# Strassen's seven products in the value projection of an encoder's first attention layer

## The chip, the cores and the metric

One core of a Trainium2 chip runs the whole program in one launch. The metric is the device time of one execution in microseconds (us), the median over the runs; one more execution was taken with the hardware profiler.

## The reference

The kernel computes a two-layer encoder on 256 tokens of width 2048, in f32. The first layer is neighbourhood attention with 12 heads of 128 columns, with 4 cross-attention heads into 256 memory tokens beside them; the second has grouped-query attention in place of the neighbourhood one. Each layer ends with a squared-ReLU MLP of width 8192. Cut to the first layer's mixer:

```python
m = rms_norm(mem, mem_norm)
n = rms_norm(h, attn_norm[0])
z = n @ a_w_in[0]                                   # 2048 x (3*1536 + 512)
q, k, v, qm = jnp.split(z, [1536, 3072, 4608], axis=-1)
mix = neighbourhood_attention(q, k, v, a_rpb[0])    # 12 heads, softmax(q k^T * scale + bias + mask) v
km, vm = jnp.split(m @ w_mem_kv[0], 2, axis=-1)
cross = memory_attention(qm, km, vm)                # 4 heads, softmax(qm km^T * scale) vm
h = h + jnp.concatenate([mix, cross], axis=-1) @ w_o[0]
h = h + jnp.square(jax.nn.relu(rms_norm(h, mlp_norm[0]) @ w_up[0])) @ w_down[0]
```

The change concerns `v`, 256 x 1536, of `n @ a_w_in[0]`.

## The kernel before, in words

**Numbers.** Each f32 operand is split into a rounded part (`hi`, made by ScalarE) and the rest (`lo`, a subtraction on VectorE); `split` (L478 to L481) does both. A product is then three matmuls: hi by hi, hi by lo, lo by hi.

**The plan.** All weights come in chunks of 128 x 2048 values (1 MB) through three raw buffers. A chunk is worked off in two halves of 1024 columns, each split into a ring of four `hi` and four `lo` buffers, three halves ahead of their use. The plan, a list of chunks, is built in the order of the computation; `run_all` goes through it half by half, and after every half `tick` (L290) issues what `later` (L287) had put off by a number of halves. From this a scheduler makes the instruction order of each engine when the program is built. An engine works through its own order and never past an instruction that still waits.

**Two kinds of chunk.** An S chunk makes the 128 columns of one head's query, key or memory query: the weights are stationary (128 x 128) and 256 tokens move, 16 blocks by three matmuls (L385), into one PSUM bank, `ps_s`. An M chunk is four blocks of the value or output projection: the activations are stationary and 512 weight columns move, 4 blocks by 2 token halves by three matmuls (L362, L365, L366), into two banks, `ps_m`. PSUM has eight banks; four are for such sums (`acc`) and four for the attention's own tiles (`att`).

**The first layer's part.** Once the memory's keys and values are there, the plan holds 4 memory-query chunks, and then three groups (`GH`) of four heads. A group is 4 M chunks for the values of its four heads (256 x 512), then a query and a key chunk for each head. When a query chunk is done, `a_q_done` scales it by 1/rms of the token out of PSUM (`summed`, L525, on VectorE, which frees the bank) and splits it; `a_k_done` does the same for the key and starts the attention of that head at the next tick. `a_v_done` scales and splits the group's values (L670 on ScalarE, L671 on VectorE, `va`).

**An attention** has four steps, put off by 1, 2, 4 and 5 ticks. `attend`: scores by six matmuls (L537 to L539), bias added (L546), the maximum (L548), the exponential on ScalarE, the reciprocal of the sum (L553), and the scaling by it, two instructions on VectorE (L555). `turned`: two transposes on VectorE (L592) and a DMA. `halved`: the split of the probabilities `pT_t`. `attend3`: six matmuls with the values (L611 to L613), and the split of the result into `cat`.

**Later parts** are the output projection, and the MLP, which already works with seven products for eight there, with its sums of weights by GpSimd's accumulating DMAs (L1073) and by VectorE (L1076).

Of the kernel before, what the change touches and what calls it, by code (L numbers as in the profile page):

```python
# [10 lines left out]
F32 = mybir.dt.float32  # L11
# [6 lines left out]
P = 128  # L18
D = 2048
# [39 lines left out]

LONGER = {"hi": 128, "lo": 128}  # L60

# [86 lines left out]


class Grain:  # L150


    def __init__(self, run, after=None, load=None, pre=None, prep=None, ahead=(8, 5, 3)):
# [4 lines left out]
def encoder_kernel(ctx: ExitStack, tc: tile.TileContext, t: dict, out: bass.AP):  # L158
# [35 lines left out]
    def open_work():  # L194
        at.work = opened("work", side="right", bufs=2)

    open_sums()
    open_ring()
    open_work()

    first = const.tile([P, GAINS + NT * D], F32, name="first")
    gains, mem0 = first[:, :GAINS], first[:, GAINS:]
    h = mem0.rearrange("p (a b) -> p a b", a=NT)
    raws = [at.ring.tile([P, CH], F32, tag="raw", bufs=3, name=f"raw{c}") for c in range(FIRST_CHUNKS)]


    def load_mem(j):
        s = slice(GAINS + j * 512 if j else 0, GAINS + (j + 1) * 512)  # L210
        nc.sync.dma_start(first[:, s], t["mem_rest"][j - 1] if j else t["mem_first"])
# [26 lines left out]
    def gain(which, k):  # L238
        return gains[:, which * KT + k : which * KT + k + 1]

# [149 lines left out]
    def begin():  # L390

        box["memT"] = at.cat.tile([P, KT, 512], F32R, tag="cat", name="memT")
        tiles = {}
        for w in plan[:FIRST_CHUNKS]:
# [134 lines left out]
    def attend(qT, kT, bias=None):  # L529
# [120 lines left out]
    def get(name):  # L650
        return lambda: box[name]
# [14 lines left out]
    def head_of(v, hd):  # L666
        return lambda part, kt: v[:, part, kt, hd * HD : (hd + 1) * HD]

# [81 lines left out]

    def x_load():
        for i in range(NT):
            pin(nc.sync.dma_start(h[:, i, :], t["x"][i * P : (i + 1) * P, :]))
        box["xT"] = []
        for a in range(2):
            y = at.work.tile([P, 8, SEQ], F32, tag="l4", name="xT")
            pin(nc.sync.dma_start(y.rearrange("p a b -> p (a b)"), t["xT"][:, a * XW // 2 : (a + 1) * XW // 2]))
            box["xT"].append(y)

# [12 lines left out]
    def x_norm(j):  # L772
        if j == 0:
            box["nT"] = wide("nT0", 480)
        for k in (2 * j, 2 * j + 1):
            split_pair(box["nT"], box["xT"][k // 8][:, k % 8, :], G_A0, k)

# [20 lines left out]
    def a_k_done(hd):  # L798
        def f(w):
            k = at.work.tile([P, 512], F32R, tag="b_y2", name="kT")  # L800
            s = summed(w.ps, "k", box["x_row"])
            split(k[:, :SEQ], k[:, SEQ:], s)
            b = at.work.tile([P, BJ * GRID_W], F32, tag="b_o", bufs=3, name="bias")
            nc.sync.dma_start(b, t["bias"][hd])
            attention([(box.pop(("q", hd)), k, b, head_of(box["v", hd // GH], hd % GH), hd, box["cat"])], 1)
        return f
# [10 lines left out]

    for hd in range(NMH):
        add_s(t["w_aqm"][hd], get("nT"), a_qm_done(hd))
# [26 lines left out]
    def o_done(layer, nb):  # L846
# [40 lines left out]
        def f(w):  # L887
            if nb == 0:
                closed("work")
                at.side = opened("side", side="right")  # L890
# [289 lines left out]
    def plain_grains(layer, nb, at_chunk):  # L1180
# [19 lines left out]
        def begin():  # L1200
            if nb == REST[0]:
                closed("ps_sums")
                open_sums(layer)
# [290 lines left out]
    later(21, x_load)  # L1494
    for j in range(8):
        later(24 + j, x_norm, j)
    later(25, x_stats)
    run_all()
# [27 lines left out]
def m_chunks(w):  # L1526

    k, n = w.shape
    x = w.reshape(k // D, 4, 4, P, n // 512, 512).transpose(0, 4, 1, 3, 2, 5)
    return np.ascontiguousarray(x).reshape(-1, P, CH)  # L1530

# [113 lines left out]
```

## Time and profile before

| | before |
|---|---|
| median of 3 runs | 2002.28 us (2002.08 to 2002.89) |
| the profiled execution's own time | 2002.73 us |
| its span, first to last instruction | 2001.0 us |
| mean granted TensorE clock | 0.999 |
| TensorE (PE) busy | 1989.8 us |
| VectorE (DVE) busy | 1718.8 us |
| ScalarE (ACT) busy | 1329.9 us |
| GpSimd (POOL) busy | 123.0 us |

The first layer's projections and attention lie at 95 to 334 us of the span.

Times in the profile are microseconds from the span's start. PE is TensorE, PEld its weight loads, DVE is VectorE, ACT ScalarE. A row of a group gives line, engine, operation, result and operand by the names in the program, the shape, the count, then busy time and mean duration in ns, then the idle time just ahead of these instructions. Matmuls overlap in the pipeline, so that their pitch, from start to start, tells what one costs, and not its duration.

### The profile page before, as it was taken

How to read it: one execution, taken by the hardware profiler on the slowest of the kernel's cores; microseconds unless marked ns; L12 is line 12 of the kernel's file. 1: busy time of each engine (PE TensorE's matmuls, PEld its weight loads, DVE VectorE, ACT ScalarE, POOL GpSimd, SP SyncE). 2: the span in 40 equal slices, each digit the busy share in tenths (PEclk: the TensorE clock that was granted, in tenths of full speed). 3: DMA queues.
4: the chain of work that ended last, by engine and by line, in shares of the span. 5: the costliest groups of instructions: out<-in, count | busy, mean ns of one | idle time of the engine just before them, and what ended most of it. 6: DMA issues, size and time to landing. Idle time of an engine off the chain costs nothing.

```text
span 2001.0 us, 32691 instructions
## 1 busy us (share of the span) xinstructions
PE 1989.8 (99%) x12920; PEld 1806.7 (90%) x12920; DVE 1718.8 (86%) x2080; ACT 1329.9 (66%) x1849; POOL 123.0 (6%) x145
## 2 busy tenths in 40 slices
PE   9999999999999999999999999999999999999998
PEld 8999999899999999999998888889999999999997
DVE  6777777589998999999999779778998999999997
ACT  6655555477777777677766556667776777777774
POOL 0000000000000000000000001000000000000000
PEclk9999999999999999999999999999999999999999
DMA  7866655767777777777666765568777777777772
GB/s 294 310 196 207 209 198 191 257 205 233 239 225 231 232 234 237 237 229 227 213 226 208 238 222 171 190 197 259 229 223 239 226 226 238 233 236 234 220 235 102
DMA packets 105562, 448.02 MB, mean 224 GB/s; under 512 B 10944, under 2 KB 38336, under 8 KB 58048
## 3 DMA queue, kind: packets, MB, share of 16 engines
q1 hardware_dynamic: 88416, 414.99, 59.2%
q0 software_dynamic: 16704, 30.42, 9.5%
q8 instruction: 101, 1.65, 0.3%
q10 hardware_dynamic: 288, 0.52, 0.1%
q14 instruction: 53, 0.43, 0.1%
HBM read 398.17 MB, written 4.19 MB: 201 GB/s over the span
## 4 chain that ended last, share of the span: by engine, by line
PE 98%; DVE 1%; issue 0%; DMA 0%; ACT 0%; SPq 0%; DVEq 0%; POOLq 0%; POOL 0%; ACTq 0%
PE ps_u L385 35%; PE ps_s L385 10%; PE p L1106 9%; PE p L1104 9%; PE p L1107 9%; PE ps_m L362 8%; PE ps_m L365 8%; PE ps_m L366 8%; PE sc_ps L538 0%; PE av L612 0%; PE sc_ps L539 0%; PE sc_ps L537 0%; PE av L611 0%; PE av L613 0%; DMA raw<-in_w_first 0%
## 5 line engine op out<-in xcount | busy, mean ns | idle before, releaser
L385 PE MATMUL ps_u<-hT,uh 128*128 128x256 f32 x3812 | 663.6, 276 | 0.0
L385 PEld LDWEIGHTS ps_u<-hT,uh 128*128 128x128 f32 x3812 | 578.9, 188 | 5.5
L385 PE MATMUL ps_u<-hT,ul 128*128 128x256 f32 x1960 | 541.5, 276 | 0.0
L480 ACT ACTIVATE uh<-raw_U 128x1024 fp32r<-128x1024 f32 x262 | 276.7, 1058 | 209.3 <-PE ps_u L385 195.7
L385 PEld LDWEIGHTS ps_u<-hT,ul 128*128 128x128 f32 x1960 | 368.0, 188 | 0.0
L481 DVE TENSOR_TENSOR lo<-raw,hi 128x1024 fp32r<-128x1024 f32 (+1 forms) x215 | 254.7, 1190 | 101.2 <-ACT hi L480 100.1
L481 DVE TENSOR_TENSOR ul<-raw_U,uh 128x1024 fp32r<-128x1024 f32 x262 | 318.4, 1219 | 15.6 <-ACT uh L480 15.4
L480 ACT ACTIVATE hi<-raw 128x1024 fp32r<-128x1024 f32 (+1 forms) x215 | 221.6, 1036 | 162.1 <-PE ps_m L366 86.7
L481 DVE TENSOR_TENSOR tl<-t,th 128x2048 fp32r<-128x2048 f32 x116 | 265.6, 2290 | 71.4 <-ACT th L480 71.0
L480 ACT ACTIVATE th<-t 128x2048 fp32r<-128x2048 f32 x116 | 222.7, 1920 | 117.4 <-PE p L1107 114.8
L481 DVE TENSOR_TENSOR bl<-b,bh 128x1536 fp32r<-128x1536 f32 x116 | 203.2, 1752 | 0.0
L1104 PE MATMUL p<-th,a_s 128*128 128x512 f32 x464 | 181.2, 391 | 0.0
L1106 PE MATMUL p<-tl,a_s 128*128 128x512 f32 x464 | 181.0, 390 | 0.0
L1107 PE MATMUL p<-th,a_s 128*128 128x512 f32 x464 | 180.5, 389 | 0.0
L480 ACT ACTIVATE bh<-b 128x1536 fp32r<-128x1536 f32 x116 | 172.4, 1486 | 7.9
L1073 POOL DMA_DIRECT2D t<-b x116 | 101.0, 871 | 1143.9 <-ACT t L1072 1060.7
L385 PE MATMUL ps_s<-nT,hi 128*128 128x256 f32 x896 | 154.7, 276 | 0.0
L1107 PE MATMUL p<-bh,a_s 128*128 128x512 f32 x348 | 136.2, 391 | 0.0
L1106 PE MATMUL p<-bl,a_s 128*128 128x512 f32 x348 | 135.7, 390 | 0.0
L385 PEld LDWEIGHTS ps_s<-nT,hi 128*128 128x128 f32 x896 | 135.5, 188 | 0.2
L1104 PE MATMUL p<-bh,a_s 128*128 128x512 f32 x348 | 135.4, 389 | 0.0
L385 PE MATMUL ps_s<-nT,lo 128*128 128x256 f32 x448 | 123.7, 276 | 0.0
(296 smaller groups left out, 3590.7 us busy)
## 6 DMA issues: line engine op xcount, KB each, us to landing
raw_U<-in_w_up SPq DMA_DIRECT2D x128, 1024.0 KB, 5.5
b<-in_w_pair SPq DMA_DIRECT2D x116, 1024.0 KB, 5.7
raw<-in_w_o SPq DMA_DIRECT2D x32, 1024.0 KB, 5.0
t<-b POOLq DMA_DIRECT2D x116, 256.0 KB, 5.2
raw<-in_w_b SPq DMA_DIRECT2D x21, 1024.0 KB, 5.2
raw<-in_w_av SPq DMA_DIRECT2D x12, 1024.0 KB, 4.9
raw<-in_w_aq SPq DMA_DIRECT2D x12, 1024.0 KB, 4.9
raw<-in_w_ak SPq DMA_DIRECT2D x12, 1024.0 KB, 4.8
```

The costliest lines, as they stand in the source:

```text
L362: first = nc.tensor.matmul(ps, ah, hi[:, s], start=st, stop=False)
L365: nc.tensor.matmul(ps, ah, lo[:, s], start=False, stop=False)
L366: final = nc.tensor.matmul(ps, al, hi[:, s], start=False, stop=sp)
L385: ins = nc.tensor.matmul(ps, x, acts[:, k, part], start=k == n == 0, stop=k == KT - 1 and n == 2)
L480: first = nc.scalar.activation(dst_hi, src, AF.Copy)
L481: return first, nc.vector.tensor_tensor(dst_lo, src, dst_hi.bitcast(F32), op=ALU.subtract)
L1073: nc.gpsimd.dma_start(s[:, 3, :], b[:, 1, :], accum_op=ALU.add)
L1104: ins = nc.tensor.matmul(ps, a[:, 0, ai, :], hi[:, s], start=begins, stop=False)
L1106: nc.tensor.matmul(ps, a[:, 0, ai, :], lo[:, s], start=False, stop=False)
L1107: nc.tensor.matmul(ps, a[:, 1, ai, :], hi[:, s], start=False, stop=ends)
```

## The change

**The products.** A 512-row, 512-column piece of the value weights is taken as two pairs of row blocks by two halves of 256 columns. For each pair the 2 x 2 block product (token halves by row blocks, row blocks by column halves) is made with Strassen's seven products `p1` to `p7`, each 128 tokens x 128 rows x 256 columns, in place of eight. A chunk has two such pairs, so 7 x 2 x 3 = 42 matmuls of 256 columns in place of 24 of 512. The seven products of a group add up over its four chunks in four banks, `ps_v`, two products to a bank.

**The operands.** Four of the products need sums of activations: `x_sums` makes them, one call for each of the four row ranges (four additions of 256 columns and a split of 1024). Four need sums of weights: `pre` makes them for each chunk with one ScalarE copy, two GpSimd accumulating DMAs of 256 KB and two VectorE additions of 512 columns. What is split for a chunk is the raw 2048 columns (half chunk one: `p3`, `p1`, `p2`, `p5`) and 1536 columns of sums (half chunk two: `p7`, `p6`, `p4`).

**The results.** `values_done` combines the products of a group out of PSUM by one ScalarE copy and seven VectorE additions of 256 columns (`v_c`), then scales and splits as before (now L693, L694).

**The order of the plan.** The value chunks of a group no longer stand ahead of it: of the 24 half chunks (three groups of four chunks, in the order 2, 0, 1, 3) one stands behind each of the 28 memory-query, query and key chunks in turn, two behind the fifth and the sixth, until they are used up.

**PSUM.** In the first layer `acc` has five banks and `att` three. While a group's values are open, four of the five hold `ps_v`, and one is left for `ps_s`.

**Besides.** In the first layer the attention's scaling goes from VectorE to ScalarE. The activations are normed in pairs of blocks, by ScalarE and then a split. `x` is loaded after its transposed copy, and once more, 2 MB, after the last group's values, since its room holds sums of activations in between. The unused columns behind `hi` and `lo` shrink from 128 and 128 to 32 and 64.

The core of the diff:

```diff
-        for x in ("acc", "att")[:: 1 if layer else -1]:
-            setattr(at, x, opened(f"ps_{x}", space=bass.MemoryType.PSUM, bufs=4))
+        for x, n in (("acc", 5 - layer), ("att", 3 + layer))[:: 1 if layer else -1]:
+            setattr(at, x, opened(f"ps_{x}", space=bass.MemoryType.PSUM, bufs=n))
...
-            nc.vector.tensor_scalar(sc[:, s, :], sc[:, s, :], rs[:, s : s + 1], None, op0=ALU.mult)
+            if box["layer"]:
+                nc.vector.tensor_scalar(sc[:, s, :], sc[:, s, :], rs[:, s : s + 1], None, op0=ALU.mult)
+            else:
+                nc.scalar.activation(sc[:, s, :], sc[:, s, :], AF.Copy, scale=rs[:, s : s + 1])
...
+    def x_sums(c):
...
+        for n, a, b, op in ((0, x[:, :, 0], x[:, :, 2], ALU.subtract), (1, x[:, :, 0], x[:, :, 1], ALU.add),
+                            (2, d[:, :, 0], x[:, :, 1], ALU.add), (3, x[:, :, 3], d[:, :, 2], ALU.subtract)):
+            nc.vector.tensor_tensor(d[:, :, n], a, b, op=op)
+        split(res[:, :, 0], res[:, :, 1], d)
...
-    def a_v_done(g):
-        def f(w):
-            box["v", g] = values("l4", "va")
-            put_values(box["v", g], w.ps, box["x_col"])
-        return f
+    PARTS = (("p3", "p1", "p2", "p5"), ("p7", "p6", "p4"))
...
+    def value_grains(g, c, begins, ends):
...
+        def pre():
+            b = own["b"].rearrange("p (a b) -> p a b", a=4)
+            s = own["t"] = at.spare.tile([P, 3, 512], F32, tag="sums", name="v_t")
+            nc.scalar.activation(s[:, 2, :], b[:, 2, :], AF.Copy)
+            nc.vector.tensor_tensor(s[:, 0, :], b[:, 3, :], b[:, 0, :], op=ALU.add)
+            nc.gpsimd.dma_start(b[:, 3, :], b[:, 1, :], accum_op=ALU.add)
+            nc.vector.tensor_tensor(s[:, 1, :], s[:, 0, :], b[:, 1, :], op=ALU.add)
+            nc.gpsimd.dma_start(s[:, 2, :], s[:, 1, :], accum_op=ALU.add)
...
+        def run(n):
+            if begins and n == 0:
+                box["v_ps"] = [at.acc.tile([P, 512], F32, tag="acc", name="ps_v") for _ in range(4)]
+            for m in range(2):
+                hi, lo = own.pop((n, m))
+                for q in range(2):
+                    for a, name in enumerate(PARTS[n][2 * m : 2 * m + 2]):
...
+                        for part, x, st, sp in ((0, hi, begin and half == 0, False), (0, lo, False, False),
+                                                (1, hi, False, end)):
+                            ins = nc.tensor.matmul(ps, left(name, q, part), x[:, s], start=st, stop=sp,
+                                                   skip_group_check=True)
...
+    def values_done(g):
...
+        nc.scalar.activation(c[:, 0, 0], p["p1"], AF.Copy)
+        for d, x, y, op in ((c[:, 1, 0], p["p2"], c[:, 0, 0], ALU.add), (c[:, 1, 1], p["p6"], c[:, 0, 0], ALU.subtract),
+                            (c[:, 0, 1], c[:, 1, 1], p["p7"], ALU.subtract), (c[:, 0, 0], c[:, 0, 1], p["p4"], ALU.add),
+                            (c[:, 0, 1], p["p5"], c[:, 0, 1], ALU.subtract),
+                            (c[:, 1, 1], c[:, 1, 1], p["p5"], ALU.subtract), (c[:, 1, 1], c[:, 1, 1], p["p3"], ALU.add)):
+            nc.vector.tensor_tensor(d, x, y, op=op)
+        box["v", g] = values("l4", "va")
+        put_values(box["v", g], [c[:, i].rearrange("p a b -> p (a b)") for i in range(NT)], box["x_col"])
+        if g == NH // GH - 1:
+            h_load()
...
-    for g in range(NH // GH):
-        add_m([t["w_av"][g * 4 + c] for c in range(4)], parts_of("nT"), a_v_done(g))
-        for hd in range(g * GH, (g + 1) * GH):
-            add_s(t["w_aq"][hd], get("nT"), a_q_done(hd))
-            add_s(t["w_ak"][hd], get("nT"), a_k_done(hd))
+    CHUNKS = (2, 0, 1, 3)
+    with_values = [x for g in range(NH // GH) for n, c in enumerate(CHUNKS) for x in value_grains(g, c, n == 0, n == 3)]
...
+    for n, (src, done) in enumerate(projections):
+        add_s(src, get("nT"), done)
+        for _ in range(1 + (n in (4, 5))):
+            if with_values:
+                plan.append(with_values.pop(0))
```

**The order of the instructions, before and after.** Each engine's order is fixed when the program is built. Numbers behind a name tell one buffer from another; `x2` stands for two instructions that follow each other.

On TensorE, before, at the key chunk `ps_s_1866` of the second head (its key is `kT_1921`) the next chunk `ps_s_1961` follows, and the head's scores `sc_ps_1937` stand at that next chunk's end:

```order
L385 MATMUL ps_s_1961<-nT0_920,hi_1893 128x256 x2
L611 MATMUL av_1928<-pT_t_1822,va_1635 128x256
L537 MATMUL sc_ps_1937<-kT_1921,qT_1855 128x256
L538 MATMUL sc_ps_1937<-kT_1921,qT_1855 128x256
L539 MATMUL sc_ps_1937<-kT_1921,qT_1855 128x256
...
L612 MATMUL av_1928<-pT_t_1822,va_1635 128x256
L613 MATMUL av_1928<-pT_t_1822,va_1635 128x256
L385 MATMUL ps_s_1961<-nT0_920,lo_1894 128x256
L385 MATMUL ps_s_2033<-nT0_920,hi_1957 128x256 x2
```

After, the second head's key chunk is `ps_s_2099` and its key `kT_2160`; the half chunk of values behind it works on `ps_v_2065` and `ps_v_2066`:

```order
L404 MATMUL ps_s_2099<-nT0_926,hi_2059 128x256 x2
L404 MATMUL ps_s_2099<-nT0_926,lo_2060 128x256
L557 MATMUL sc_ps_2167<-kT_2160,qT_2045 128x256
L558 MATMUL sc_ps_2167<-kT_2160,qT_2045 128x256
L559 MATMUL sc_ps_2167<-kT_2160,qT_2045 128x256
...
L559 MATMUL sc_ps_2167<-kT_2160,qT_2045 128x256
L882 MATMUL ps_v_2065<-hi_2091,left_1028 128x256
L882 MATMUL ps_v_2065<-lo_2092,left_1028 128x256
```

The scores stand directly behind the last matmul of the key that they need, and ahead of the half chunk of values.

On TensorE after the change, in the steady part of the second group, the key chunk `ps_s_2565` is followed by the next head's query chunk `ps_s_2689`:

```order
L404 MATMUL ps_s_2565<-nT0_926,lo_2521 128x256
L404 MATMUL ps_s_2565<-nT0_926,hi_2520 128x256 x2
L404 MATMUL ps_s_2565<-nT0_926,lo_2521 128x256
L404 MATMUL ps_s_2689<-nT0_926,hi_2598 128x256 x2
L404 MATMUL ps_s_2689<-nT0_926,lo_2599 128x256
```

Two S chunks in a row stood there before as well; now `ps_v` holds four of the five banks, so that both are in the same bank. Eight such pairs stand in the order.

On VectorE, before, where group 0's values (`va_1635`) are made out of `ps_m`:

```order
L481 TENSOR_TENSOR lo_1643<-raw_1640,hi_1642 128x1024
L481 TENSOR_TENSOR cat0_1154<-av_1557,cat0_1154 128x256
L671 SCALAR_TENSOR_TENSOR va_1635<-ps_m_1472,x_col_965,va_1635 128x512
L671 SCALAR_TENSOR_TENSOR va_1635<-ps_m_1473,x_col_965,va_1635 128x512
L481 TENSOR_TENSOR lo_1672<-raw_1640,hi_1671 128x1024
```

After, with the query `q_s_2046` of the second head, taken out of `ps_s_1986`, among the combinations `v_c_1964`:

```order
L903 TENSOR_TENSOR v_c_1964<-v_c_1964,ps_v_1227 128x256
L545 SCALAR_TENSOR_TENSOR q_s_2046<-ps_s_1986,x_row_999 128x256
L903 TENSOR_TENSOR v_c_1964<-ps_v_1225,v_c_1964 128x256
L903 TENSOR_TENSOR v_c_1964<-v_c_1964,ps_v_1225 128x256
L501 TENSOR_TENSOR lo_2018<-raw_2015,hi_2017 128x1024
L903 TENSOR_TENSOR v_c_1964<-v_c_1964,ps_v_1224 128x256
L501 TENSOR_TENSOR lo_2060<-raw_2015,hi_2059 128x1024
L501 TENSOR_TENSOR pT_t_1937<-pT_t_1937 128x512
L501 TENSOR_TENSOR qT_2045<-q_s_2046,qT_2045 128x256
L694 SCALAR_TENSOR_TENSOR va_1973<-v_c_1964,x_col_993,va_1973 128x512 x2
```

Three of the seven combinations and both writes of `va_1973` now stand behind the reading of a query chunk that ends one S chunk later than the group's products. The first matmuls with these values, `av_2050`, stand on TensorE directly behind that S chunk, `ps_s_1986`.

More of the change, by code (lines that the diff above doesn't have):

```diff
@@ L58 @@
 ENTRY_AT = 192
[L60 removed]
+LONGER = {"hi": 32, "lo": 64}
+LEFT = 16
 COPY_AT = 384
@@ L147, in __getitem__ @@
         return self.rest[:, s.start - P : s.stop - P] if s.start else self.first
+class Rows:
+    def __getitem__(self, key):
+        return self.now[key]
 class Grain:
+    kind, last_block = "G", False
     def __init__(self, run, after=None, load=None, pre=None, prep=None, ahead=(8, 5, 3)):
@@ L238, in gain @@
     def gain(which, k):
-        return gains[:, which * KT + k : which * KT + k + 1]
+        src = first[:, LEFT:] if which == G_MEM else gains
+        return src[:, which * KT + k : which * KT + k + 1]
     box: dict = {"layer": 0}
@@ L392, in begin @@
         box["memT"] = at.cat.tile([P, KT, 512], F32R, tag="cat", name="memT")
+        later(1, lambda: nc.scalar.activation(gains, first[:, LEFT : LEFT + GAINS], AF.Copy))
         tiles = {}
@@ new lines, in values_done @@
+    def values_done(g):
+        p = {name: box["v_ps"][bank][:, half * SEQ : (half + 1) * SEQ] for name, (bank, half) in PLACES.items()}
+        c = at.work.tile([P, NT, 2, SEQ], F32, tag="pT", name="v_c")
+        nc.scalar.activation(c[:, 0, 0], p["p1"], AF.Copy)
[7 more added lines that the diff above has]
+        if g == NH // GH - 1:
+            h_load()
@@ L888, in f @@
             if nb == 0:
+                if not layer:
+                    closed("spare")
                 closed("work")
@@ L1494, in encoder_kernel @@
     later(21, x_load)
-    for j in range(8):
-        later(24 + j, x_norm, j)
-    later(25, x_stats)
+    for n, j in enumerate((4, 5, 0, 1, 2, 3, 6, 7)):
+        later(24 + n, x_norm, j)
+    for n, c in zip((27, 29, 31, 34), CHUNKS):
+        later(n, x_sums, c)
+    later(26, x_stats)
     run_all()
```

96 lines of the change are left out of this document (77 added, 19 removed).

## The prediction

> **What bounds the kernel now.** I read the page first (the span, the engines' busy time and the chain that ended last).
>
> ```profile
> span 2001.0 us, 32691 instructions
> PE 1989.8 (99%) x12920; PEld 1806.7 (90%) x12920; DVE 1718.8 (86%) x2080; ACT 1329.9 (66%) x1849; POOL 123.0 (6%) x145
> PEclk9999999999999999999999999999999999999999
> PE 98%; DVE 1%; issue 0%; DMA 0%; ACT 0%; SPq 0%; DVEq 0%; POOLq 0%; POOL 0%; ACTq 0%
> ```
>
> TensorE sets the end: 99% busy and 98% of the chain, at full granted clock in every slice. Only fewer TensorE microseconds can shorten this kernel, and every wait of TensorE lengthens it. Then the windows, for the first layer's projections and for a stretch of its MLP (columns: PE, PEld, DVE, ACT, POOL, clock, DMA share, GB/s):
>
> ```profile
> 95.00:334.00 239.00, 239.00 (x1808) 227.40 (x1808) 176.36 (x272) 125.13 (x202) 0.00 (x0) 1.00 0.62 206
> 600.00:900.00 300.00, 300.00 (x2023) 275.30 (x2022) 277.18 (x289) 214.68 (x249) 25.32 (x29) 1.00 0.75 233
> ```
>
> In the stage of the change TensorE is busy in 239.00 of 239.00 us: no wait is there to be removed. VectorE has 176.36 of 239 (74%). In the MLP it has 277.18 of 300 (92%), and TensorE still never waits, so that a load of 92% can be carried if the order leaves room.
>
> **What the products save.** The matmuls' pitch, from the list of TensorE's instructions in order of time (start, duration):
>
> ```profile
> 136.03 0.39 PE L366 MATMUL ps_m<-hi,nT 128*128 128x512 f32 x1
> ...
> 136.71 0.39 PE L366 MATMUL ps_m<-hi,nT 128*128 128x512 f32 x1
> ...
> 150.85 0.28 PE L385 MATMUL ps_s<-nT,lo 128*128 128x256 f32 x1
> 150.96 0.39 PE L385 MATMUL ps_s<-nT,hi 128*128 128x256 f32 x2
> 151.19 0.28 PE L385 MATMUL ps_s<-nT,lo 128*128 128x256 f32 x1
> ```
>
> Three matmuls of 512 columns take 136.71 − 136.03 = 0.68 us, .2267 each; three of 256 take 151.19 − 150.85 = 0.34, .1133 each: exactly half. The value projection has 12 chunks x 24 = 288 of the one kind, 65.3 us, and gets 12 x 42 = 504 of the other, 57.1 us. **Term 1: −8.2 us.** If the new matmuls ran at the pitch of the scores (rows below: .117), 504 x .004 = 2 us of it would be lost; I take the S chunk's pitch, since shape and way of loading are its own.
>
> The Trainium skill, "TensorE: Matmul & The Clock Gate", section "Wait — 56ns, not 53.3ns?", gives each warm matmul a fixed part of about 2.5 ns beside its columns. By it the 216 matmuls more would take an estimated .5 us of the saving back; the two pitches above, exactly 2 to 1, show no such part.
>
> **What the sums cost.** VectorE's durations, in a stretch where it runs without gaps:
>
> ```profile
> 244.48 0.69 DVE L546 TENSOR_TENSOR sc<-sc_ps,bias 128x512 f32<-128x512 f32 x1
> 245.19 0.42 DVE L525 SCALAR_TENSOR_TENSOR q_s<-ps_s,x_row 128x256 f32<-128x256 f32 x1
> 245.53 1.22 DVE L481 TENSOR_TENSOR lo<-raw,hi 128x1024 fp32r<-128x1024 f32 x1
> 246.66 0.68 DVE L548 TENSOR_REDUCE nm<-sc 128x2 f32<-128x512 f32 x1
> 247.26 0.41 DVE L481 TENSOR_TENSOR cat<-av,cat 128x256 fp32r<-128x256 f32 x1
> 247.59 0.41 DVE L481 TENSOR_TENSOR qT<-q_s,qT 128x256 fp32r<-128x256 f32 x1
> ...
> 249.24 1.15 DVE L592 STREAM_TRANSPOSE sc_t<-sc 128x256 f32<-128x256 f32 x2
> 250.31 1.18 DVE L481 TENSOR_TENSOR lo<-raw,hi 128x1024 fp32r<-128x1024 f32 x1
> ```
>
> From start to start: .34 for 256 columns, .60 for 512, 1.14 for 1024, 1.07 for both transposes. One head of the changed stage (query, key, one value chunk) then asks of VectorE: S splits 4 x 1.14 = 4.6; value splits 3 x 1.14 + .60 = 4.0; sums of weights 2 x .60 = 1.2; q, k and `cat` 5 x .34 = 1.7; the rest of the attention 3 x .60 + 1.07 + .2 for the reciprocal (a rounded-up .17) = 3.1; a quarter of `values_done`, (7 x .34 + 2 x .7)/4 = .9. Together 15.5 us. TensorE needs 96 x .1133 + 42 x .1133 + 12 x .12 = 17.1 us. That is 91%, the MLP's load: VectorE alone doesn't become the bound. In the stretch from the first memory query to the second head's query the order holds, with the sums of activations, 25 subtractions of 1024, 22 operations of 512, 26 of 256, 10 transposes and 5 reciprocals, 56.9 us, against 58.1 of TensorE (6 S chunks of 5.44, 4 value chunks of 4.76, 54 attention matmuls): 98%, tight.
>
> The accumulating DMAs and the reload lie beside this:
>
> ```profile
> L1073 POOL DMA_DIRECT2D t<-b x116 | 101.0, 871 | 1143.9 <-ACT t L1072 1060.7
> t<-b POOLq DMA_DIRECT2D x116, 256.0 KB, 5.2
> ```
>
> 24 issues of .87 us on a GpSimd that is idle here (0.00 in the window), each landing in 5.2 us. A value chunk comes round every 17 us, its raw data three steps ahead of use. Two DMAs in turn make 2 x (5.2 + .9) = 12 us, which the rest of a period covers with 5 us left; without that cover each chunk would cost the excess. The 2 MB of `x` at the end wait behind nothing that TensorE needs before the output projection, and the ScalarE copies and scalings go to an engine with 125 of 239 us busy. All three at nothing.
>
> **What the order costs.** Before, a head's scores stand amid the chunk after the next matmuls, so that nothing waits:
>
> ```profile
> 231.40 0.28 PE L385 MATMUL ps_s<-nT,hi 128*128 128x256 f32 x1
> 231.52 0.28 PE L538 MATMUL sc_ps<-kT,qT 128*128 128x256 f32 x1
> 231.64 0.28 PE L539 MATMUL sc_ps<-kT,qT 128*128 128x256 f32 x1
> ...
> 231.99 0.28 PE L539 MATMUL sc_ps<-kT,qT 128*128 128x256 f32 x1
> 232.11 0.28 PE L385 MATMUL ps_s<-nT,hi 128*128 128x256 f32 x1
> 232.31 0.69 DVE L546 TENSOR_TENSOR sc<-sc_ps,bias 128x512 f32<-128x512 f32 x1 [0.35 <-PE sc_ps L539]
> 5.20 0.69 DVE L481 TENSOR_TENSOR lo<-raw,hi 128x512 fp32r<-128x512 f32 x1
> 5.95 0.39 PE L385 MATMUL ps_s<-memT,lo 128*128 128x256 f32 x1 [0.23 <-DVE lo L481]
> ```
>
> These give the two handovers: from TensorE's last matmul to a waiting VectorE 232.31 − 231.99 = .32, which is .20 after the next matmul could have started (231.99 + .12); from VectorE's end, 5.20 + .69 = 5.89, to TensorE at 5.95, .06. After the change TensorE, which never steps past a waiting instruction, meets four kinds of wait; each is a sum of these rows, with VectorE and ScalarE just in time.
>
> A. *Scores directly behind the chunk that they need.* For the second key (the first place of the order) VectorE reads `k_s` (.34), subtracts `lo_2186` (1.14, it stands between) and then `kT` (.42): .20 + .34 + 1.14 + .42 + .06 = 2.16, less .12 for the one matmul that goes ahead, 2.0. The first key has a 512 between: 1.5. The first memory query has .34, 1.14, .34 between: .20 + .34 + 1.82 + .42 + .06 less two matmuls, 2.6. The second has 1.14, 1.14, .60 between, less eight matmuls: 3.0. At the fifth key `av_3032` stands ahead of the scores, and ahead of its `pT_t` (.69) stand 1.14 and .60: .20 + .34 + 1.74 + .69 + .06 less two matmuls, 2.8. Sum 11.9.
>
> B. *One bank for two S chunks.* TensorE may not start the second before VectorE has read the first: .20 + .42 + .06 = .68, eight times, 5.4.
>
> C. *Group 0's values behind a query* (the third place). From the end of `ps_s_1986`: .20, then .34 for the query, 3 x .34 + 2 x 1.14 + .60 + .34 in VectorE's order, .66 for the first `va` and .75 for the second to be there, .06:
>
> ```profile
> 215.33 1.40 DVE L671 SCALAR_TENSOR_TENSOR va<-ps_m,x_col,va 128x512 fp32r<-128x512 f32 x2
> ```
>
> 6.2 us, less .5 for the matmuls of the first half: 5.7.
>
> D. *`ps_s_1816`* (first key) needs a `lo` that stands seven places behind the first query's reading on VectorE: .20 + .34 + 1.14 + .60 + 1.07 + .34 + .60 + .34 + 1.22 + .06 = 5.9, of which 31 matmuls between hide 3.5: 2.4.
>
> **Term 2: +11.9 + 5.4 + 5.7 + 2.4 = +25.4.** VectorE isn't just in time, though: it finishes what it has in hand. The trace of before has no such wait, so I bound it: nothing, or one 1024 subtraction (1.14) at each of the 15 waits, 17. I take half of one at each, as nearest to a queue 91 to 98% full. **Term 3: +8.5.** A later wait also gives VectorE time to catch up, which is why I don't go above it.
>
> Sum on the profiled execution: its own time 2002.73 − 8.2 + 25.4 + 8.5 = 2028.4. That execution was .45 over the median of the runs, so 2028.0.
>
> **The rivals.**
>
> *Faster: the waits are covered.* If the handovers of A, C and D overlapped with work that the order hides from me (matmuls of other banks ahead of the waiting ones), only B would be left: 2002.3 − 8.2 + 5.4 = 1999.5; with B covered too, 1994.1. It decides from the point where all waits together are under 8.2. Against it: each chain above begins with the last matmul of a chunk and ends at the very next instruction. 5%.
>
> *VectorE as the bound in the tight stretch alone.* If scores and values waited little but the 98% stretch could be run only at the MLP's 92%, it would take 56.9/.92 = 61.8 in place of 58.1, +3.7: 2002.3 − 8.2 + 3.7 = 1997.8. For it: the MLP row. Against it: the same as above. 4%.
>
> *The granted clock falls after long waits.* C, the second memory query and the fifth key with lateness hold waits of 3 to 6 us, which the trace of before has nowhere; its clock is full in all 40 slices. If it halved for one S chunk after each of two such waits, 2 x 5.44 = 11 us more: 2039.0. The Trainium skill, the same page, section "What's actually happening" in Part 1, has such a gate, with a window of about 3.4 us; the trace of before, without such an idle stretch, can't show it. 10%.
>
> *The forecast*, 80%; 1% for something else, on the slow side.
>
> **The numbers.** 2028.0. Low: term 3 at nothing and a third of term 2 covered, 2028.0 − 8.5 − 8.5 = 2011.0; high: term 3 whole (+8.5) and the scores' pitch (+2), 2038.5, drawn out to the clock's rival, 2039.0. About 4.0 us (0.2%) either way is what a measurement of this kernel can tell from no change. Of the two fast rivals (9%) I give half to each side of that bound: faster .05, same .04, slower .91.
>
> **What would show it.** In TensorE's waits of the changed kernel: the five scores of A behind VectorE's or ScalarE's `kT`, `qmT`; eight waits of about .7 for VectorE's `k_s` or `qm_s`; one of about 6 for `va`; TensorE's busy time less by 8, VectorE in the stage near 91%. I am wrong if these waits sum to under 12 us, if the matmuls at L882 have a pitch other than .113, or if the clock leaves 1.00.

## The result, and the profile after

The changed kernel takes 2049.64 us, median of 4 runs (2049.11 to 2050.81), against 2002.55 us of the kernel before beside it: a ratio of 1.0236, 95% interval 1.0218 to 1.0254. It is slower, as forecast, but by 47 us where 26 were forecast, and outside the range (2011 to 2039). Its page, the rows that answer to those shown of before:

```profile
span 2047.6 us, 33383 instructions
PE 2006.2 (98%) x13136; PEld 1826.6 (89%) x13136; DVE 1760.5 (86%) x2126; ACT 1376.8 (67%) x1933; POOL 144.3 (7%) x169
PEclk9988999999999999999999999999999999999999
PE 92%; DVE 3%; DMA 2%; issue 1%; ACT 1%; SPq 0%; DVEq 0%; POOL 0%; POOLq 0%; ACTq 0%
```

TensorE is busy for 16.4 us more, although it has 8 us less to do: two slices with a granted clock of 8 tenths are new. The chain has VectorE, DMA and ScalarE in it now. Nearly all of it is in the stage of the change (the window's columns: PE, PEld, DVE, ACT, POOL, clock, DMA share, GB/s; then TensorE's waits there: us in total, times, longest):

```profile
95.00:345.00 250.00, 219.00 (x1735) 213.72 (x1734) 187.27 (x272) 141.31 (x233) 19.01 (x22) 0.95 0.67 203
```

```profile
PE sc_ps L557 <- ACT qmT L500: 6.5, 2, 4.3
PE ps_s L404 <- DVE k_s L545: 4.6, 6, 1.5
PE av L634 <- ACT pT_t L500: 3.9, 2, 3.4
PE av L634 <- ACT va L693: 3.3, 1, 3.3
PE sc_ps L557 <- ACT kT L500: 3.2, 2, 1.9
PE ps_s L404 <- DVE qm_s L545: 3.0, 2, 1.8
PE av L635 <- DVE pT_t L501: 2.1, 3, 0.9
PE ps_s L404 <- DVE lo L501: 2.1, 1, 2.1
...
```

These are the forecast's waits by name: scores for `qmT` and `kT`, eight S chunks for the reading of their bank (`k_s` six times, `qm_s` twice), one for `lo`, `av` for `va` and `pT_t`. VectorE is busy in 187.27 of 250 us, 75%: it is not the bound.

The longest wait, 4.33 us at the first memory query, has a cause of its own. The query's last matmul starts at 101.57; behind it, on ScalarE and VectorE:

```profile
102.34 2.00 ACT L500 ACTIVATE hi<-raw 128x1024 fp32r<-128x1024 f32 x2 [4.01 <-DMA raw<-in_w_aqm]
105.25 0.42 DVE L545 SCALAR_TENSOR_TENSOR qm_s<-ps_s,x_row 128x256 f32<-128x256 f32 x1
```

ScalarE waits 4.01 us for the next chunk's weights to land, VectorE's subtractions stand behind ScalarE's rounding, and the query is read at 105.25, some 3.4 us later than in the forecast's chain.

The second head's key, in TensorE's and VectorE's lists (start, duration):

```profile
201.00 0.28 PE L404 MATMUL ps_s<-nT,lo 128*128 128x256 f32 x1
202.62 0.38 PE L557 MATMUL sc_ps<-kT,qT 128*128 128x256 f32 x1 [1.34 <-ACT kT L500]
203.90 0.38 PE L558 MATMUL sc_ps<-kT,qT 128*128 128x256 f32 x1 [0.90 <-DVE kT L501]
204.12 0.34 PE L559 MATMUL sc_ps<-kT,qT 128*128 128x256 f32 x1
```

```profile
201.32 0.42 DVE L545 SCALAR_TENSOR_TENSOR k_s<-ps_s,x_row 128x256 f32<-128x256 f32 x1 [0.63 <-PE ps_s L404]
202.29 1.23 DVE L501 TENSOR_TENSOR lo<-raw,hi 128x1024 fp32r<-128x1024 f32 x1 [0.55 <-ACT hi L500]
203.43 0.42 DVE L501 TENSOR_TENSOR kT<-k_s,kT 128x256 fp32r<-128x256 f32 x1
```

This is the forecast's chain: VectorE reads at 201.32, .32 after the last matmul; the subtraction of 1024 that stands between starts .55 late, because ScalarE's rounding was late; `kT` follows at 203.43 and TensorE goes on at 203.90. From 201.00 to 204.12 there are three matmuls, .34 us of work: 2.8 us lost, forecast 2.0 and a part of term 3.

Now the clock, in windows of 3.41 us (busy us of TensorE with its matmuls first, the granted clock third from the end):

```profile
101.83:105.25 3.42, 0.01 (x1) 0.00 (x0) 1.81 (x4) 2.00 (x2) 0.00 (x0) 0.99 1.07 352
105.25:108.66 3.41, 1.59 (x5) 1.30 (x6) 2.62 (x7) 1.48 (x2) 0.00 (x0) 0.50 0.70 231
108.66:112.07 3.41, 3.41 (x17) 3.41 (x17) 1.93 (x3) 1.35 (x5) 0.00 (x0) 0.50 0.67 276
132.60:136.00 3.40, 1.63 (x14) 1.46 (x13) 2.50 (x4) 2.00 (x3) 0.00 (x0) 1.00 0.74 284
136.00:139.40 3.40, 3.40 (x32) 3.40 (x31) 0.68 (x2) 1.39 (x2) 0.00 (x0) 1.00 0.76 251
170.07:173.48 3.41, 1.54 (x10) 1.34 (x11) 3.38 (x6) 1.51 (x3) 0.32 (x1) 1.00 0.74 240
173.48:176.89 3.41, 3.41 (x19) 3.41 (x17) 1.78 (x4) 1.47 (x4) 1.41 (x2) 0.50 0.89 206
```

A window at full clock in which TensorE was busy for .01 or 1.54 us is followed by one at half clock (17 to 19 matmuls where 32 fit); one with 1.63 us is not. The window with 1.59 us is itself at half clock, and another follows it. The edges lie on one grid: 112.07, 125.76, 176.89 and 207.65 are 4, 15 and 9 times 3.41 apart. Eight windows of the stage are at half clock, behind the five waits of A and behind C.

Where the 46.6 us of span went. Adding up, for each matmul of the stage, the time to the next one's start less .1133 us per 256 columns:

| | forecast | measured |
|---|---|---|
| products (term 1) | −8.2 | −8.2 (no row against it) |
| A, scores behind their chunk | 11.9 | 19.8 |
| B, one bank, eight times | 5.4 | 8.9 |
| C, group 0's values | 5.7 | 5.6 |
| D, `ps_s_1816` | 2.4 | 2.4 |
| one more wait, for `pT_t` | | 0.7 |
| lateness (term 3, in A to D when measured) | 8.5 | |
| matmuls at half clock | 0, a rival of 10% | 9.7 |
| matmuls at .118 where .1133 was taken | 0, bound 2 | 4.4 |
| the rest: 1.2 ahead of the stage, .5 behind the output projection, 1.6 not assigned | | 3.3 |
| sum | 25.7 | 46.6 |

The waits come to 37.4 us where terms 2 and 3 had 33.9. The rows for half clock and for the pitch of .118 are what the forecast lacked.

### The profile page after: what moved, and what is told of

Its sections match the earlier page's. It is cut to its first block, busy times and chain, and to the rows that moved or that the text cites. A ratio compares the mean times of both kernels' runs of the same rounds, so it can differ in the third digit from the quotient of the medians.

```text
span 2047.6 us, 33383 instructions
## 1 busy us (share of the span) xinstructions
PE 2006.2 (98%) x13136; PEld 1826.6 (89%) x13136; DVE 1760.5 (86%) x2126; ACT 1376.8 (67%) x1933; POOL 144.3 (7%) x169
## 4 chain that ended last, share of the span: by engine, by line
PE 92%; DVE 3%; DMA 2%; issue 1%; ACT 1%; SPq 0%; DVEq 0%; POOL 0%; POOLq 0%; ACTq 0%
PE ps_u L404 34%; PE p L1230 9%; PE p L1228 9%; PE p L1231 9%; PE ps_s L404 7%; PE ps_m L381 6%; PE ps_m L385 6%; PE ps_m L384 6%; PE ps_v L882 2%; DVE lo L501 1%; DMA mem_k<-km_w 1%; DMA raw<-in_w_aqm 1%; ACT hi L500 0%; PE av L635 0%; PE av L636 0%
## 5 line engine op out<-in xcount | busy, mean ns | idle before, releaser
L404 PE MATMUL ps_s<-nT,hi 128*128 128x256 f32 x896 | 159.9, 279 | 7.5 <-DVE k_s L545 4.6
```

Source lines behind the costliest of these rows:

```text
L404: ins = nc.tensor.matmul(ps, x, acts[:, k, part], start=k == n == 0, stop=k == KT - 1 and n == 2)
```

## The experiments

The theory: **order**. TensorE loses its time at handovers that the order of the instructions forces, each priced as above, and to the half clock that follows where they leave a window too empty. Its rivals: **load** (VectorE's added work makes the waits, wherever they stand) and **products** (the value matmuls themselves don't save). The kernel before ran beside all of them, 2002.5 to 2002.8 us.

### scores_behind: before, with the scores behind their chunk

```diff
-        products(w.ps, w.acts(), k0, nk, hi, lo)
+        products(w.ps, w.acts(), k0, nk, hi, lo, keep_order="nT" in box and not box["layer"])
```

> The kernel before, with its products for eight, four banks and no sums, but with the S chunks' matmuls of the first layer kept in the order of the plan: the scores of 9 heads and 3 memory heads then stand directly behind the chunk that they need. Theory (order): 12 waits of .20 + .34 + 1.14 + .42 + .06 = 2.2 us, some less, 20 to 28 us, and after the longer ones a halved clock, 0 to 20 us more: 2022 to 2050, granted clock in that stage under 1.00. Rival (load): VectorE has 74% in that stage here, so that it catches up, under 2008.

Measured: 2044.39 us, ratio 1.0210 (1.0194 to 1.0226). TensorE's waits in the stage, and its window:

```profile
PE sc_ps L537 <- ACT kT L480: 9.1, 9, 1.4
PE sc_ps L538 <- DVE kT L481: 7.8, 9, 0.9
PE sc_ps L537 <- ACT qmT L480: 4.5, 3, 1.7
PE sc_ps L539 <- DVE qmT L481: 1.1, 2, 0.8
```

```profile
95.00:375.00 280.00, 257.26 (x1807) 240.34 (x1806) 182.38 (x275) 125.98 (x203) 0.00 (x0) 0.96 0.52 175
```

Twelve heads, 22.5 us of idling (29 from start to start), and 12 us of matmuls at half clock: +42, without a single product, sum or bank of the change. VectorE has 65% there. Order holds, load falls for this kernel. Two windows of this run show that the busy time alone doesn't tell which window is followed by a slow one:

```profile
263.59:267.00 3.41, 1.81 (x13) 1.42 (x12) 2.23 (x4) 1.11 (x3) 0.00 (x0) 1.00 0.33 91
267.00:270.41 3.41, 3.41 (x18) 3.41 (x18) 2.18 (x6) 1.10 (x4) 0.00 (x0) 0.50 0.82 334
```

Here 1.81 us were too little, where 1.63 were enough in the changed kernel. The matmuls that start in a window tell it better: 11 here, 12 there. Over the windows at full clock of eleven runs (from 60 us on, a matmul of 512 columns counted twice), all 46 with up to 11 starts were followed by a halved one and none with 13 or more; of the three with 12, two were.

### one_bank: before, with one bank for S chunks in a row

```diff
         def start(w):
+            if "nT" in box and not box["layer"] and plan[plan.index(w) - 1].acts is acts:
+                w.ps = box["ps_s"][:, :SEQ]
+                return
...
```

> The kernel before, in which the S chunks of the first layer that follow each other all use one PSUM bank; nothing else changed. Theory (order and banks): three groups have seven such handovers and the memory queries some, 20 in all, each .20 + .42 + .06 = .68 us: +13.6, about 2016, and as each wait is short the clock stays at 1.00. Rival (load): VectorE has a quarter of its time free, within 4 us of before.

Measured: 2022.49 us, ratio 1.0101 (1.0088 to 1.0115), +20 where 13.6 were expected. The clock row stays at 1.00.

```profile
PE ps_s L385 <- DVE k_s L528: 5.5, 9, 0.6
PE ps_s L385 <- DVE q_s L528: 4.9, 9, 0.6
PE ps_s L385 <- DVE qm_s L528: 1.1, 2, 0.6
```

Twenty waits, as counted; from start to start they cost 14.9 us, .74 each, and one for `pT_t` .9. The other 4 are S matmuls, .1165 on the mean, in a kernel whose buffers are those of before. About 1.8 of it lies directly behind the handovers, where the first matmul takes .08 to .11 longer; of the rest about a third run at .117 to .119, so that the slower pitch comes with such handovers as well.

### sums_alone: before, with the work of the sums on scratch

```diff
                 box["weights"] = split(*tiles[hf], src)
+                if "a_v_done" in w.done.__qualname__:
+                    more(src)
...
+    def more(src):
+        a = at.spare.tile([P, 3, 768], F32, tag="more", name="more")
+        nc.vector.tensor_tensor(a[:, 0, :512], src[:, :512], src[:, 512:], op=ALU.add)
+        nc.scalar.activation(a[:, 1], src[:, :768], AF.Copy)
+        nc.vector.tensor_tensor(a[:, 2], src[:, 256:], a[:, 1], op=ALU.subtract)
...
```

> The kernel before with most of the changed kernel's additional work on VectorE and ScalarE for the values, on scratch: for each half chunk of values one addition of 512, a rounding of 768 on ScalarE and a subtraction of 768 on VectorE, 24 of each, about 36 us more of VectorE (74% to 89% of the stage); the results are not used, the values are made by eight products as before, and the sums of activations and the accumulating DMAs are left out. Theory (order): no wait of TensorE, within 4 us of before. Rival (load): VectorE's work alone makes TensorE wait, 2012 or more.

Measured: 2002.52 us, ratio 1.0001 (0.9991 to 1.0010).

```profile
95.00:333.00 238.00, 238.00 (x1802) 226.49 (x1801) 207.48 (x317) 142.27 (x226) 0.00 (x0) 1.00 0.61 206
```

VectorE at 207.48 of 238, 87%, and TensorE waits nowhere. Work alone costs nothing while the order leaves it room.

### later_all: after, with the attention one tick later

```diff
-            attention([(box.pop(("q", hd)), k, b, head_of(("v", hd // GH), hd % GH), hd, box["cat"])], 1)
+            attention([(box.pop(("q", hd)), k, b, head_of(("v", hd // GH), hd % GH), hd, box["cat"])], 2)
...
-            attention([(q, box["km"][:, hd, :], None, head_of(box["vm"], hd), NH + hd, box["cat"])], 1)
+            attention([(q, box["km"][:, hd, :], None, head_of(box["vm"], hd), NH + hd, box["cat"])], 2)
```

> The changed kernel with the first layer's attention steps put off by one tick more (2, 3, 5 and 6 in place of 1, 2, 4 and 5; two numbers); products, sums, banks and all other work are unchanged. Theory (the order: handovers that TensorE must wait out, and a halved clock after long ones): the scores now stand behind a half chunk of values, 14 to 24 matmuls, 1.6 to 2.7 us, which covers .20 + .34 + .42 + .06 and most of a subtraction; no two S chunks in one bank stand next to each other any more. The waits of over 1 us go, the clock stays at 1.00, and the products' 8.2 us are seen: 1994 to 2001. Rival (VectorE's load, 91 to 98%): the work is the same, so the waits come up at other places, 2025 or more. Rival (the products don't save): no long waits, but 2002 or more, and a pitch above .115 at the value matmuls.

Measured: 2018.11 us, ratio 1.0082 (1.0069 to 1.0094).

```profile
PE ps_s L404 <- DVE rs L573: 3.2, 2, 1.6
PE ps_s L404 <- DVE qm_s L545: 3.0, 1, 3.0
...
```

Two numbers take 31.5 of the 47 us away, with the same work: the waits of the stage fall from 31 us to 8. But no expectation was met: 1994 to 2001 was too low, 2025 too high, and of the third, the pitch of the value matmuls came true (.117, above .115) but not the absence of long waits. What is left in the stage are other waits (8 us idle, 9.9 from start to start), one window at half clock (1.4) and S and value matmuls at about .1165 (6 us more than at .1133).

### slots_alone and later_slots: the buffers

```diff
-LONGER = {"hi": 128, "lo": 128}
+LONGER = {"hi": 32, "lo": 64}
```

> The kernel before with nothing but the changed kernel's lengths of the ring's buffers (32 and 64 columns behind hi and lo for 128 and 128). Theory (buffers): S chunks at .118, 28 chunks of 48 matmuls times .005, +6 us or more, 2008 to 2011. Rival (value matmuls): S chunks at .1133, within 2 us of 2002.5.

Measured: 2008.53 us, ratio 1.0028 (1.0018 to 1.0039). Two stretches of S chunks (start, duration):

```profile
163.46 0.28 PE L385 MATMUL ps_s<-nT,lo 128*128 128x256 f32 x1
...
166.30 0.28 PE L385 MATMUL ps_s<-nT,lo 128*128 128x256 f32 x1
...
177.91 0.28 PE L385 MATMUL ps_s<-nT,lo 128*128 128x256 f32 x1
...
179.95 0.28 PE L385 MATMUL ps_s<-nT,lo 128*128 128x256 f32 x1
```

From 163.46 on 24 matmuls take 2.84 us, .118 each, and from 177.91 on 18 take 2.04, .1133 each, both at full clock and without a wait: the S chunk has a second pitch. This one line of the change costs 5.7 us by itself. The time lies in the expected range, but by luck: S chunks at .118 throughout would have cost over 6 us in the stage, and only 2.4 arose there, with a mean of .115; the other 3.3 lie ahead of the stage and behind it.

The line in later_slots, on top of later_all, and its pad:

```diff
-LONGER = {"hi": 32, "lo": 64}
+LONGER = {"hi": 64, "lo": 64}
...
-        for pool in (at.ring, at.cat):
+        for pool in (at.ring,):
```

> The run later_all with the ring's hi buffers longer by 32 columns (64 behind hi and 64 behind lo, as equal as they were in the kernel before; one unused pad of 256 bytes is left out to make room). All hi and lo buffers then start at the same address modulo 256 bytes, while in the changed kernel every second hi buffer lies 128 bytes off. In later_all the S chunks between half chunks of values run at a pitch of .118 in place of .1133, which costs 4 to 6 us. Theory (buffers): with equal buffers all S chunks and values run at .1133 to .1135, 5 to 7 us less than later_all, 2011 to 2013. Rival (the value matmuls leave TensorE in the slower pitch, whatever the buffers): within 2 us of later_all's 2018, S chunks behind values still at .118.

Measured: 2015.52 us, ratio 1.0065 (1.0051 to 1.0079), 2.6 less than later_all, between the two expectations, with intervals that overlap. S matmuls at full clock still have .115 on the mean. Equal buffers don't bring the pitch back between value matmuls; what sets it stays open.

### clock_alone: waits of known length

```diff
+    for again in range(4):
+        for steps in STEPS:
...
+            for k in range(many):
+                nc.tensor.matmul(ps, w, last, start=k == 0, stop=k == many - 1)
+            nxt = a[:, 1 + n % 2]
+            for k in range(steps):
+                nc.vector.tensor_scalar(nxt if k == steps - 1 else junk, ps, 0.001, None, op0=ALU.mult)
+            last = nxt
...
+STEPS = (1, 2, 3, 4, 5, 6, 7, 8, 10, 12, 14, 16)
```

> A measurement, not the encoder: only 48 bursts of 120 to 148 matmuls of 128 x 128 x 256, each waiting for a chain of VectorE operations on the burst before (1 to 16 operations of 256 columns, waits of about .6 to 6 us), four rounds of twelve lengths; no chunk of weights, no attention, the output is not the encoder's. Theory (clock by windows): bursts behind waits under about 1.5 us keep their pitch; behind waits of over 2 to 3.4 us the matmuls run at twice the pitch until the next edge of a grid of 3.41 us, so that the slow stretch is up to 3.4 us long and starts and ends at multiples of 3.41 us. Rival (restart): every wait, short or long, is followed by the same number of slow matmuls. Rival (no clock): the pitch after a wait is the pitch before it, and the slow stretches in the changed kernel come from its operands.

Two of its 47 waits, and the windows behind them:

```profile
76.78 3.38 PE L176 MATMUL ps<-a,w 128*128 128x256 f32 x26 [1.76 <-DVE a L179]
...
97.02 4.16 PE L176 MATMUL ps<-a,w 128*128 128x256 f32 x20 [2.22 <-DVE a L179]
```

```profile
78.40:81.80 3.40, 3.40 (x30) 3.40 (x29) 0.00 (x0) 0.00 (x0) 0.00 (x0) 1.00 0.00 0
97.00:101.00 4.00, 3.98 (x20) 3.98 (x21) 0.00 (x0) 0.00 (x0) 0.00 (x0) 0.57 0.00 0
```

Behind waits of .52 to 1.76 us the clock stays whole, 16 times of 16; behind 2.22 us it is halved 3 times of 4, behind 2.68 twice of 4, behind 3.14 us and more 23 times of 23. Added up over half-microsecond windows, the clock lost behind one wait is 1.71, 3.42 or 5.12 us and nothing else: half of one, two or three windows of 3.41. The matmuls lose that only as far as they fill these windows, so that 1.71 us a window is the most that one costs. The clock theory holds, the two rivals fall.

### sums_gpsimd, loads_first, both_mended: what is left

```diff
-            nc.vector.tensor_tensor(d[:, :, n], a, b, op=op)
+            nc.gpsimd.tensor_tensor(d[:, :, n], a, b, op=op)
```

> The run later_slots with the sixteen additions of the activations' sums on GpSimd in place of VectorE. In later_slots VectorE is busy in all of 110 to 120 us, and TensorE waits 3.1 us there for the reading of a memory query's bank, after which the clock is halved for 46 matmuls (5 us). Theory (tight stretch): with 5.4 us less on VectorE that wait and the slow matmuls after it are gone, 2007 to 2010. Rival (the loads): the wait comes from a chunk of weights that lands late and stays, within 2 us of later_slots' 2015.5.

Measured: 2016.52 us (1.0054 to 1.0087): no gain. The wait grew from 3.1 to 4.9 us. VectorE, ScalarE and GpSimd in that stretch:

```profile
107.45 0.96 DVE L501 TENSOR_TENSOR qmT<-qm_s,qmT 128x256 fp32r<-128x256 f32 x1
```

```profile
108.96 2.87 POOL L823 TENSOR_TENSOR x_d<-xT 128x256 f32<-128x256 f32 x2
113.02 1.07 ACT L500 ACTIVATE left<-x_d 128x1024 fp32r<-128x1024 f32 x1 [4.91 <-POOL x_d L823]
```

An addition takes GpSimd up to 1.4 us, four times VectorE's .34, ScalarE waits 4.91 us for them, and VectorE's own split of 256 beside them takes .96 in place of .42.

```diff
...
+        def fetch():
+            tiles["raw"] = at.ring.tile([P, CH], F32, tag="raw", bufs=3, name="raw")
+            box["load"] = nc.sync.dma_start(tiles["raw"], w.src)
+
+        if "a_q_done" in w.done.__qualname__ or "a_k_done" in w.done.__qualname__:
+            return [Grain(lambda: run(0), None, fetch, None, lambda: prep(0), (5, 5, 3)),
+                    Grain(lambda: run(1), after, None, None, lambda: prep(1))]
```

> The run later_slots with the loads of the first layer's query and key chunks issued five half chunks ahead of use in place of three, so that the key's load no longer stands on SyncE's queue behind the four DMAs of the probabilities, which wait for VectorE's transposes. In later_slots TensorE waits twice, 1.8 and 2.1 us, at 225 and 263 us, for VectorE behind a late key chunk. Theory (queue): both waits gone, 4 us less, about 2011. Rival (tight stretch only): within 2 us of 2015.5, since those waits come from VectorE's load.

Measured: 2010.70 us, ratio 1.0038 (1.0023 to 1.0053), 4.8 less than later_slots; the four executions lie from 2007.84 to 2011.57, all under later_slots' lowest, 2015.06. The key's load now stands ahead of the four DMAs of the probabilities (first row later_slots, then loads_first):

```profile
215.82 0.52 SPq L289 DMA_DIRECT2D raw<-in_w_ak  x1
205.70 0.33 SPq L327 DMA_DIRECT2D raw<-in_w_ak  x1
```

The two waits named `rs` are gone. What is left, in the fastest of the four executions, the profiled one:

```profile
PE ps_s L411 <- DVE qm_s L552: 3.1, 1, 3.1
...
```

> The runs sums_gpsimd and loads_first together. Theory: the two gains add, 2003 to 2007, and in the best case the 8.2 us of the products come out under the kernel before, 1998 or less. Rival (the load moves the wait on): no better than the better of the two alone.

Measured: 2014.31 us (1.0044 to 1.0074), no better than loads_first alone, as the rival had it.

### last_sums_later and sums_early: the tight stretch

```diff
-    for n, c in zip((27, 29, 31, 34), CHUNKS):
+    for n, c in zip((27, 29, 31, 35), CHUNKS):
```

> The run loads_first with the sums of the last row range (four additions and a split of 1024) put off by one tick, so that in VectorE's order they no longer stand ahead of the second memory query's reading out of its bank. Of loads_first's 8 us over the kernel before, 3.2 are TensorE's wait there and 2 to 4 the halved clock behind it. Theory (tight stretch, order again): 2.5 us of VectorE's work less ahead of the reading, so that the wait falls under 1 us, the clock stays at 1.00 and 4 to 6 us are gone, 2004 to 2007. Rival (a late chunk of weights holds VectorE up): within 2 us of 2010.7.

Measured: 2006.51 us, ratio 1.0018 (1.0008 to 1.0027).

```profile
PE av L641 <- ACT pT_t L507: 1.3, 2, 0.7
PE ps_s L411 <- DVE lo L508: 0.9, 1, 0.9
PE ps_s L411 <- DVE qm_s L552: 0.6, 1, 0.6
...
```

The wait of 3.1 us is .6, the stage's waits come to 3.0 us, its clock is 1.00. All ten executions (2004.98 to 2007.62) lie under loads_first's lowest; the 95% intervals of the two ratios just overlap.

The kernel is still 3.8 us slower than before, and in the stage of the change nothing is left of the products' saving. From its first `ps_s` to the MLP's first matmul, which is the same work but for the values, the profile shows 328.3 us, and 328.1 in the kernel before. The 8.2 us go into its waits, about 4.4 from start to start, and into S and value matmuls above .1133, about 3.9.

```diff
-    later(21, x_load)
+    later(18, x_load)
...
-        later(24 + n, x_norm, j)
+        later(21 + n, x_norm, j)
-    for n, c in zip((27, 29, 31, 34), CHUNKS):
+    for n, c in zip((24, 26, 28, 36), CHUNKS):
```

> The run loads_first with x's load, the norm and the sums of the first three row ranges three ticks earlier, in the memory's stage where VectorE has a quarter of its time free, and the last range's two ticks later. Theory (tight stretch): the wait of 3.1 us at the second memory query and the halved clock behind it are gone, 2003 to 2007. Rival (the memory's stage): the earlier work makes TensorE wait in the memory's value projection instead, start of the stage 1 us or more later, 2009 or more.

Measured: 2008.08 us (1.0018 to 1.0040), 2.6 less than loads_first with intervals that overlap, between the two expectations. Both were right in part. The stage's first matmul starts at 100.15 us in place of loads_first's 95.86, behind a wait of 1.9 us for VectorE in the memory's value projection and one window at half clock there, as the rival had it. And the stage with the output projection then takes 325.9 us, 2.2 less than in the kernel before: here a part of the products' saving shows, and it is paid for ahead of the stage. No version was found that beats the kernel before.

## Why the prediction was right and wrong

**What bounds the kernel**: right. TensorE's busy time and waits make the span; VectorE, at 75% of the longer stage where 91% were forecast, is no bound.

**Term 1**: the count is right, its pitch was too good. Some value matmuls do run at .1133, but most near .118 (.117 on the mean), and many S chunks behind them too: 4.4 us of the 8.2 are lost again. The bound of 2 us was drawn for the value matmuls alone, and the shorter buffers, which the prediction left at nothing without a reason, cost 5.7 us when put alone into the kernel before.

**Term 2**: right by kind and place. The chains C and D came out to about a tenth. A took 8 us and B 3.5 more than their sums, which is what term 3 was for.

**Term 3**: near in size, 8.5 us for 12.0 (with the wait that was not named), but partly by luck. Twice in B VectorE did finish what it had in hand, as the prediction reasons. The largest parts have another cause: the first memory query's, because its successor's weights land late (6.0 for 2.6 us), and the fifth key's, where ScalarE waits for the DMA of `pT_t` (5.0 for 2.8).

**The step that failed** is putting the halved clock at nothing in the sum. It stands there as a rival only, "the granted clock falls after long waits", at 10%, with two stretches of 5.44 us. It was no alternative to the forecast but a part of it: A and C by the prediction's own sums put waits of 1.5 to 5.7 us into the stage, and scores_behind and clock_alone show that waits of about 2 us and more can empty a window of 3.41 us far enough. Eight windows at half clock cost 9.7 us in matmuls. That this is near the rival's 11 us is luck: it had two events of 5.44 us, and there are eight windows of 1.2 us on the mean, each 1.71 at most by clock_alone. With the clock and the pitch as terms the sum would have been 25.7 + 9.7 + 4.4 = 40, and a range as wide as the one given would have held the time. That is after the fact, and 6.8 us of the 46.6 stay outside it: 3.5 of waits, and the 3.3 of the last row.

Two of the prediction's own signs of being wrong came true, the clock under 1.00 and a pitch other than .113 at the value matmuls; the third, waits under 12 us, did not.

The Trainium skill, "TensorE: Matmul & The Clock Gate", Part 1, "What's actually happening", has the free-running window of 4096 cycles, 3413 ns; the edges at multiples of 3.41 us agree with it. It speaks of an idle window. Here a window with TensorE busy for 1.54 of 3.41 us was enough, and in clock_alone single waits of 2.22 us were enough 3 times of 4, so that the waits to fear begin at about 2 us.

**The other rivals**. "Faster, the waits are covered": wrong for this kernel, but later_all shows that two numbers cover most. "VectorE as the bound in the tight stretch": not as a bound; loads_first and last_sums_later show a single wait there, made by one row range's sums (four additions and a split) that stood ahead of a reading.

**Costed at nothing**: the accumulating DMAs and the ScalarE work, rightly as far as any wait by their name shows. The loads of weights, which the prediction doesn't price, were not free: in the changed kernel one that lands late makes the longest wait, and in later_slots a key's load stood on SyncE's queue behind the DMAs of `turned`; loads_first, which mends that, is 4.8 us faster.

Still open: what puts TensorE into the pitch of .118. Buffers that are shorter and no longer equal do it alone (slots_alone; which of the two was not tried), and handovers in one bank alone do it too (one_bank); equal buffers between value matmuls didn't undo it (later_slots).

## What to carry to other kernels

A kernel whose TensorE never waits has an order that took care of it: price a change by what its new order puts directly behind a producing matmul and by the banks that it takes away, before counting matmuls. Wherever that adds waits of 2 us or more, add up to 1.71 us for each window at half clock that follows them (1.2 on the mean here), as a term of the sum. Work added to an engine with room cost nothing here (sums_alone), the place of one row range's sums in VectorE's queue cost 4 us (last_sums_later against loads_first).

## What the runs showed of the hardware that was not expected

- The clock is granted by windows of 3.41 us on a fixed grid, and a window need not be idle to be followed by a halved one: with TensorE busy for 1.54 us (changed kernel) and for 1.81 us (scores_behind) it was, with 1.63 us (changed kernel) it was not. Counted in matmuls of 256 columns that start in it, up to 11 in a window at full clock (of about 30 that fit) were always followed by a halved one, 13 or more never.
- Matmuls of 128 x 128 x 256 have two steady pitches at full clock, .1133 and .1183, for the same kind of chunk and without a wait; shorter padding behind two kinds of buffer was enough to bring the second one in (slots_alone).
- Beside additions on GpSimd VectorE slows down: .96 for .42 us (256 columns, sums_gpsimd). With GpSimd's own .7 to 1.4 us for an addition, sixteen of them moved to an idle engine made the wait that they were to shorten longer, 4.9 for 3.1 us.
